# A two-layer hybrid block: tokens before the filters, and the convolutions of both lengths as one stream

## The chip, the cores and the metric

The kernel runs on one core of one Trainium2 chip. The metric is the device time of one execution in microseconds (us). TensorE is called PE in the profile (its weight loads PEld), VectorE DVE, ScalarE ACT, GpSimd POOL; SP is the engine that only issues DMAs. SP, ACT and POOL each issue their DMAs in the order in which they stand in that engine's instruction stream.

## The reference

Two layers of a token mixer and an MLP on 512 latent tokens and 256 context tokens of width 1024. Each sub-layer is modulated: a vector c (and one for the context) is multiplied with `w_mod`, and the result scales, shifts and gates the tokens. The mixer has four groups of 256 channels: a bidirectional state-space scan (SSD), a long convolution (Hyena), windowed attention and dense attention. What the change touches is the long convolution and its filters:

```python
def hyena_seq(u, conv_w, conv_b, spec, bias):
    n = u.shape[1]
    u = dw_conv_centred(u, conv_w, conv_b).astype(jnp.float32)
    v, x1, x2 = jnp.split(u, 3, axis=-1)
    gates = (x1, x2)
    z = v
    for o in range(HY_ORDER):            # HY_ORDER = 2
        zf = jnp.fft.irfft(jnp.fft.rfft(z, n=2 * n, axis=1) * spec[:, o], n=2 * n, axis=1)[:, :n]
        z = gates[o] * (zf + z * bias[o])
    return z
```

It is computed once for the 512 latent tokens in both layers and once for the 256 context tokens in layer 0 (layer 1 leaves the context out, since only the latents are returned). `spec` is the transform of an implicit filter: a small MLP with sines over positions, times a decay, normalised. The transforms are matrix products with constant tables of cosines and sines.

## The kernel before, in words

Everything is float32 in, float32 out. Most products are made of three matmuls in a reduced format (`mm3`, lines 296 to 300): each operand is split in a high part (`hi`, line 265 on ACT or 267 on DVE) and a low rest (`lo`, line 270 on DVE), and high by high, high by low and low by high are added in PSUM.

The program is written with pools of tiles: `push` opens a pool with so many buffers a tag, `a(tag)` takes the next one, `pop` closes it, and the place of a closed pool is used again by the next pool as soon as each tile in it is done with. A planner orders the instructions on each engine; its priority is the order in which they are written. `weave` (line 203) writes several generators in turn: in each round it runs n steps (to the next n yields) of each, with n given per generator. So a larger n puts a generator's work earlier.

The beginning (`run`, from line 1334). `filter_loads`, `filter_tables` and `filter_head` load the small filter weights and the tables on the queues of SP and POOL and compute the sine MLP. `pre` loads two token tiles of 128 x 1024 and normalises them; for the first pair this is done first, for the other two pairs after the weave. The weave runs `mod_cols` (two sections of `w_mod`, eight loads of 0.5 MB each on SP's queue with six buffers `wm`, and four small matmuls for each load, lines 447 and 449) with three steps a round beside `filter_seq(0, SEQ)` with two. `filter_seq` makes, for each of two orders, four filter tiles `kd` (lines 677 to 681), their sum and difference `ko` (696), transposes and splits them into `fx` (702, 704, 705), multiplies by the tables (716) and writes the spectra to DRAM through `fk` on POOL's queue (725). For layer 0 the large length has buffers of its own (`kd0`, `ko0`, `fx0`, `fk0`, in the pool `filL`). That pool is closed after the weave, and only then the pool of the transposed tokens (`push_xt`: tiles `xl` for the latents and `xc` for the context, high and low) is opened at its place. `pre_pair` (line 583) transposes the tokens on PE (593), applies the modulation (598) and splits them into `xl` and `xc` (267, 270). After that `filter_seq(1, SEQ)`, `filter_seq(0, CTX)` and the first projection to q, k and v (`qkv_in`, tiles `pg`) are written, then `layer` for each layer.

The middle of a layer (lines 1402 to 1423): SSD, long convolution and modulation are woven. `hyena` has 12 steps in each order for 512 tokens: two of transposes (802), four of forward products with a table each (`ht`, issued on POOL's queue, line 782), a product with the spectrum (`kt`, loaded on SP's queue at 816) and a split into `hu`, four of inverse products (847) with a table each (841), and two that add z (864) and multiply by the gate (866 or 868). For 256 tokens there are one, two, two and two. In layer 0 two such generators run in the weave, with one step a round each, beside SSD (one step) and four sections of `w_mod` (two steps, loads at line 447 into three buffers `raw`, which the weight loads share). They have separate tiles (`hx`, `hu`, `hxc`, `huc`) and banks (`ph2` one, `ph3` two, `pc` one), and share three table buffers `ht`. In layer 1 there is only the long length, with six buffers `ht` and two banks `ph2`, and no modulation. Behind the stage come `w_out` (tiles `py`, weights `wx` from line 348) and the MLP.

Of the kernel before, what the change touches and what calls it, by code (L numbers as in the profile page):

```python
# [12 lines left out]
F32 = mybir.dt.float32  # L13
# [9 lines left out]
SEQ = 512  # L23
# [141 lines left out]
W0 = (3, 2)  # L165
ME = (4, 1, 2)
EN = (("dve",), ("act", "dve"), ("dve",))
W2 = (1, 1, 2, 1)
# [15 lines left out]
class K:  # L184
# [420 lines left out]
    def filter_loads(self):  # L605
# [6 lines left out]
        zf = self.zf = self.a("fh")  # L612
# [4 lines left out]
        for l in range(DEPTH):  # L617
            r = slice(64 * l, 64 * l + 64)
            nc.sync.dma_start(w12[r, 1, r], A["hy_w2"][l])
        self.w3 = self.a("fw3")  # L620
        nc.sync.dma_start(self.w3, A["hw3"])

    def filter_head(self):
# [7 lines left out]
        for i in range(2):  # L631
            dst = self.a("fh")
# [23 lines left out]
    def filter_seq(self, l, n, tabs, v=""):  # L656
# [9 lines left out]
        for o in range(2):  # L666
            ss = self.sm(4, F32, "ss")
            kds = []
            for c in range(2):
# [4 lines left out]
                for d in range(2):  # L674
# [3 lines left out]
                    t = self.a("kd" + v)[:, :n]  # L678
# [12 lines left out]
            for cs in range(2):  # L691
                X = [self.a("fx" + v, (nb, 256)) for _ in range(2)]
                for c in range(2):
                    kd = kds[c]
                    src = self.a("ko" + v)[:, :n]
# [11 lines left out]
                for kc in range(h // 128):  # L707
                    p = self.a("pmod" if not v and kc % 2 else "pf3")
# [10 lines left out]
                    kt = self.a("fk" + v, (2, 256))  # L719
# [38 lines left out]
    def hyena(self, l, n, off, YT):  # L758
# [6 lines left out]
        v = "" if big else "c"  # L765
# [4 lines left out]
        def bank(tag):  # L770
            return self.a(tag if big else "pc")
        z = [self.a("hz" + v)[:, :n] for _ in range(2)]
        for c in range(2):
            nc.sync.dma_start(z[c], self.us_d[l][c][:, off:off + n])
        for o in range(2):
            ft = {}

            def ftab(sg, tcx, hl, kc):
                i = kc if big else 0
                if i not in ft:  # L780
                    ft[i] = self.a("ht")
                    nc.gpsimd.dma_start(ft[i], A["fwd%d" % n][i])
                if big:
                    c0 = 512 * sg + 256 * tcx + 128 * hl
                else:
                    c0 = 512 * sg + 256 * hl + 128 * kc
                return ft[i][:, c0:c0 + 128]

            pq = []
            for c in range(2):  # L790
                t = tmp((2, h))
                rev = z[c][:, n - 1:h - 1:-1]
                nc.vector.tensor_tensor(t[:, 0], z[c][:, 0:h], rev, ADD)
                nc.vector.tensor_tensor(t[:, 1], z[c][:, 0:h], rev, SUB)
                pq.append(t)
            X = []
            for sg in range(2 if big else 1):
                p = bank("ph3")
                for b in range(4):
                    c = b % 2  # L800
                    src = pq[c][:, sg, 128 * (b // 2):128 * (b // 2) + 128] if big else pq[c][:, b // 2, :]
                    nc.tensor.transpose(p[:, 128 * b:128 * b + 128], src, self.ident)
                x = self.a("hx" + v, (2, 512))
                self.hi(x[:, 0], p)
                self.lo(x[:, 1], p, x[:, 0])
                X.append(x)
                yield

            def xs(sg, tcx, hl):
                c0 = 256 * (tcx if big else sg)  # L810
                return X[sg if big else 0][:, hl, c0:c0 + 256]

            uv = []
            for kc in range(nk):
                kt = tmp((2, 256))
                nc.sync.dma_start(kt, self.spec[l, n][kc].rearrange("p (s o c) -> p s o c", s=2, o=2)[:, :, o, :])
                p = bank("ph2")
                for sg in range(2):
                    for tcx in range(nt):
                        self.mm3(p[:, 256 * sg:256 * sg + 256], ftab(sg, tcx, 0, kc), ftab(sg, tcx, 1, kc),  # L820
                                 xs(sg, tcx, 0), xs(sg, tcx, 1), tcx == 0, tcx == nt - 1)
                pv = p.rearrange("p (s c) -> p s c", s=2)
                a, b = tmp((2, 256)), tmp((2, 256))
                nc.vector.tensor_tensor(a, pv, kt[:, 0:1, :].to_broadcast([128, 2, 256]), MUL)
                nc.vector.tensor_tensor(b, pv, kt[:, 1:2, :].to_broadcast([128, 2, 256]), MUL)
                nc.vector.tensor_tensor(a[:, 0], a[:, 0], b[:, 1], SUB)
                nc.vector.tensor_tensor(a[:, 1], a[:, 1], b[:, 0], ADD)
                u = self.a("hu" + v, (2, 512))
                af = a.rearrange("p s c -> p (s c)")
                self.hi(u[:, 0], af)  # L830
                self.lo(u[:, 1], af, u[:, 0])
                uv.append(u)
                yield
            if big:
                ps = [bank("ph3") for _ in range(2)]
            else:
                p = bank("pc")
                ps = [p[:, 0:n], p[:, n:2 * n]]
            for kc in range(nk):
                tb = self.a("ht")  # L840
                nc.gpsimd.dma_start(tb, A["inv%d" % n][kc])
                tb = tb.rearrange("p (a b t) -> p a b t", a=2, b=2)
                for c in range(2):
                    for sg in range(2):
# [789 lines left out]
```

## Time and profile before

| | |
|---|---|
| median of 3 runs | 1918.94 us (1918.18 to 1923.98) |
| the profiled execution | 1919.0 us |
| its span, first to last instruction | 1917.2 us |
| mean granted clock of TensorE | 0.974 |
| busy: PE, PEld, DVE, ACT, POOL | 1790.2, 1482.7, 1297.7, 836.8, 91.5 us |
| DMA | 235.16 MB, mean 123 GB/s |

The busy times of the engines lie side by side, not one after the other. A PE row is the time of pipelined matmuls with modelled ends, so rows overlap. A row of the timeline merges equal instructions that follow each other (x6), and in brackets stands for how long the engine was idle before and what ended it. The chain of waits is followed back from the last instruction.

### The profile page before, as it was taken

What the parts mean: (1) busy time and instruction counts of PE and PEld (TensorE: products, weight loads), DVE (VectorE), ACT (ScalarE), POOL (GpSimd) and SP (SyncE); (2) the same over time, 40 slices, a digit from 0 to 9 for tenths busy, and PEclk for the clock granted to TensorE, in tenths of its full rate; (3) what the DMA queues carried; (4) which work ended last, traced back from release to release, by engine and by line L of the source; (5) the groups of instructions that cost most, each with busy time, mean ns of one, the idle gap of its engine ahead of it and who ended that gap; (6) DMA issues with size and microseconds to landing.
All of it is one profiled execution on the core that took longest, in us unless ns stands there. A gap on an engine that the chain in (4) does not pass through costs nothing.

```text
span 1917.2 us, 27370 instructions
## 1 busy us (share of the span) xinstructions
PE 1790.2 (93%) x10170; PEld 1482.7 (77%) x10170; DVE 1297.7 (68%) x2897; ACT 836.8 (44%) x1804; POOL 91.5 (5%) x176
## 2 busy tenths in 40 slices
PE   6899999978879999999999998899978789999998
PEld 2688888845668888888888888888866688888886
DVE  4878888877756656676666658988878563444446
ACT  4844565536515532322222327556546263332322
POOL 0120001011000000000000000000010000000000
PEclk9999999989989999999999999999989899999999
DMA  8531121278833244333333415112183243233232
GB/s 291 187 111 53 39 74 58 69 260 272 290 107 132 93 135 136 121 107 114 121 121 121 142 47 176 45 48 89 45 273 120 74 157 113 91 99 99 88 102 85
DMA packets 137597, 235.16 MB, mean 123 GB/s; under 512 B 12466, under 2 KB 77395, under 8 KB 137464
## 3 DMA queue, kind: packets, MB, share of 16 engines
q1 hardware_dynamic: 122920, 186.12, 30.2%
q0 software_dynamic: 14544, 47.30, 7.1%
q8 instruction: 80, 1.31, 0.3%
q14 instruction: 53, 0.43, 0.1%
HBM read 206.74 MB, written 26.64 MB: 122 GB/s over the span
## 4 chain that ended last, share of the span: by engine, by line
PE 76%; DVE 9%; issue 6%; DMA 4%; ACT 4%; POOL 1%; SPq 0%; DVEq 0%; ACTq 0%; POOLq 0%
PE pg L298 19%; PE pg L299 18%; PE pg L300 18%; PE po L1294 3%; PE py L298 2%; PE py L299 2%; PE pm L1286 2%; PE py L300 2%; PE ps L1249 1%; PE ps L1250 1%; PE pm L1206 1%; PE psd L1052 1%; DMA spec<-fk 1%; POOL spec L725 1%; DMA r<-in_w_mod_dram 1%
## 5 line engine op out<-in xcount | busy, mean ns | idle before, releaser
L265 ACT ACTIVATE w<-r 128x1024 fp32r<-128x1024 f32 (+1 forms) x176 | 186.6, 1061 | 348.1 <-PE pg L300 325.1
L270 DVE TENSOR_TENSOR w<-r,w 128x1024 fp32r<-128x1024 f32 (+1 forms) x176 | 214.1, 1223 | 106.1 <-ACT w L265 105.2
L298 PE MATMUL pg<-xl,w 128*128 128x512 f32 (+1 forms) x704 | 269.5, 386 | 2.2 <-DVE ya L1311 0.9
L300 PE MATMUL pg<-xl,w 128*128 128x512 f32 (+1 forms) x704 | 269.7, 384 | 0.0
L299 PE MATMUL pg<-xl,w 128*128 128x512 f32 (+1 forms) x704 | 269.7, 384 | 0.0
L298 PE MATMUL pg<-w,H 128*128 128x512 f32 x640 | 250.1, 391 | 0.0
L299 PE MATMUL pg<-w,H 128*128 128x512 f32 x640 | 249.2, 390 | 0.0
L300 PE MATMUL pg<-w,H 128*128 128x512 f32 x640 | 249.0, 389 | 0.0
L476 DVE SCALAR_TENSOR_TENSOR x<-r,scT,x 128x512 f32<-128x512 f32 x168 | 119.1, 746 | 71.7 <-DMA r<-in_w_mod_dram 71.7
L298 PEld LDWEIGHTS pg<-xl,w 128*128 128x128 f32 x704 | 132.6, 190 | 27.7 <-issue 2.2
L300 PEld LDWEIGHTS pg<-xl,w 128*128 128x128 f32 x704 | 133.3, 189 | 22.9
L299 PEld LDWEIGHTS pg<-xl,w 128*128 128x128 f32 x704 | 133.3, 189 | 22.2 <-DVE xl L270 0.2
L298 PEld LDWEIGHTS pg<-w,H 128*128 128x128 f32 x640 | 120.1, 188 | 26.8 <-issue 1.7
L300 PEld LDWEIGHTS pg<-w,H 128*128 128x128 f32 x640 | 120.1, 188 | 25.0
L299 PEld LDWEIGHTS pg<-w,H 128*128 128x128 f32 x640 | 120.2, 188 | 24.4
L1520 ACT ACTIVATE t<-pg 128x512 f32<-128x512 f32 (+1 forms) x100 | 50.4, 506 | 198.0 <-PE pg L300 198.0
L1551 DVE TENSOR_TENSOR ya<-pg,ya 128x512 f32<-128x512 f32 x120 | 81.8, 687 | 69.0 <-PE pg L300 68.7
L1522 DVE TENSOR_TENSOR t<-t 128x512 f32<-128x512 f32 (+1 forms) x100 | 58.1, 582 | 83.7 <-ACT H L1521 83.6
L300 PE MATMUL pg<-xc,w 128*128 128x256 f32 (+1 forms) x368 | 104.4, 284 | 0.0
L298 PE MATMUL pg<-xc,w 128*128 128x256 f32 (+1 forms) x368 | 103.3, 284 | 1.1 <-ACT xc L265 1.1
L299 PE MATMUL pg<-xc,w 128*128 128x256 f32 (+1 forms) x368 | 104.1, 284 | 0.0
L298 PE MATMUL pg<-w,xl 128*128 128x256 f32 (+1 forms) x320 | 93.0, 292 | 5.4 <-ACT qk L1113 2.5
(357 smaller groups left out, 3866.1 us busy)
## 6 DMA issues: line engine op xcount, KB each, us to landing
r<-in_mlp_w_dram SPq DMA_DIRECT2D x128, 512.0 KB
r<-in_w_mod_dram SPq DMA_DIRECT2D x80, 512.0 KB
r<-in_w_in_dram SPq DMA_DIRECT2D x40, 512.0 KB
ht<-in_inv_dram POOLq DMA_DIRECT2D x20, 512.0 KB, 5.4
ht<-in_fwd_dram POOLq DMA_DIRECT2D x18, 512.0 KB, 5.4
wm<-in_w_mod_dram SPq DMA_DIRECT2D x16, 512.0 KB
r<-in_w_out_dram SPq DMA_DIRECT2D x16, 512.0 KB
xd<-x POOLq DMA_DIRECT2D x16, 512.0 KB, 3.3
```

Source lines behind the costliest of these rows:

```text
L265: self.nc.scalar.activation(dst, src, AF.Copy)
L270: self.nc.vector.tensor_tensor(dst, src, h.bitcast(F32), SUB)
L298: mm(out, ah, bh, start=first, stop=False)
L299: mm(out, ah, bl, start=False, stop=False)
L300: mm(out, al, bh, start=False, stop=last)
L476: nc.vector.scalar_tensor_tensor(acc[:, c], raw[:, k], sc, acc[:, c], MUL, ADD)
L725: nc.gpsimd.dma_start(dst, kt[:, half, :])
L1286: nc.tensor.transpose(p[:, n:n + 128], P[:, col:col + 128], self.ident)
L1294: nc.tensor.matmul(po[:, qo:qo + m], V[:, c, :], pt[:, hl, cols[j]:cols[j] + m], start=i + j == 0 and hl == 0, stop=i + j == len(kts) - 1 ...
L1520: nc.scalar.activation(r, p[:, :nn], AF.Relu)
L1522: nc.vector.tensor_tensor(r, r, r, MUL)
L1551: nc.vector.tensor_tensor(dst, p, dst, ADD)
```

## The change

Three things change.

First, the beginning. The pool of the transposed tokens is opened before the filters' and has its own place; the large filter buffers (`kd0`, `ko0`, `fk0`, `fx0`) go, and all three calls of `filter_seq` use the small ones (four `kd`, two `ko`, one `fk`, three `fx`). All three pairs of token tiles are loaded and normalised first. The weave has two generators: the tokens (both sections of `w_mod`, then `pre_pair` for the three pairs: 18 and 3 steps) with six steps a round, and the filters (loads, then tables, head and `filter_seq(0, SEQ)`) with one. The input `zf` of the filter MLP takes one of the `raw` buffers.

Second, the convolutions. `hyena` becomes one generator over both lengths, in the order: 512 order 0, 256 order 0, 512 order 1, 256 order 1, with two steps a round in layer 0. Both lengths use the same tiles `hx` and `hu`, the same banks (`ph2` two, `ph3` two, `pc` is gone) and six table buffers `ht`. Layer 1 is as it was.

Third, the attention's `sqk` has five buffers instead of four.

The body of `hyena_order` is that of `hyena` for one order, but for the lines below.

```diff
-W0 = (3, 2)
+W0 = (6, 1)
-W2 = (1, 1, 2, 1)
+W2 = (1, 1, 2, 2)
...
-        zf = self.zf = self.a("fh")
+        zf = self.zf = self.raw_p.tile([128, 1024], F32, tag="r", name=self.nm("r"))[:, :NTOK]
+        self.h1 = self.a("fh")
-            dst = self.a("fh")
+            dst = self.a("fh") if i else self.h1
...
-    def filter_seq(self, l, n, tabs, v=""):
+    def filter_seq(self, l, n, tabs, two=True):
-                    t = self.a("kd" + v)[:, :n]
+                    t = self.a("kd")[:, :n]
-                X = [self.a("fx" + v, (nb, 256)) for _ in range(2)]
+                X = [self.a("fx", (nb, 256)) for _ in range(2)]
-                    src = self.a("ko" + v)[:, :n]
+                    src = self.a("ko")[:, :n]
-                    p = self.a("pmod" if not v and kc % 2 else "pf3")
+                    p = self.a("pmod" if two and kc % 2 else "pf3")
-                    kt = self.a("fk" + v, (2, 256))
+                    kt = self.a("fk", (2, 256))
...
-    def hyena(self, l, n, off, YT):
+    def hyena(self, l, lens, YT):
+
+        self.mark("hyena")
+        zs = {}
+        for n, off in lens:
+            zs[n] = [self.a("hz" if n == SEQ else "hzc")[:, :n] for _ in range(2)]
+            for c in range(2):
+                self.nc.sync.dma_start(zs[n][c], self.us_d[l][c][:, off:off + n])
+        for o in range(2):
+            for n, off in lens:
+                yield from self.hyena_order(l, n, off, YT, zs[n], o)
+
+    def hyena_order(self, l, n, off, YT, z, o):
...
-        v = "" if big else "c"
-        def bank(tag):
-            return self.a(tag if big else "pc")
...
-                p = bank("ph3")
+            p = self.a("ph3")
...
-                x = self.a("hx" + v, (2, 512))
+            x = self.a("hx", (2, 512))
...
-                p = bank("ph2")
+            p = self.a("ph2")
...
-                u = self.a("hu" + v, (2, 512))
+            u = self.a("hu", (2, 512))
...
-                ps = [bank("ph3") for _ in range(2)]
-            else:
-                p = bank("pc")
+            ps = [self.a("ph3") for _ in range(2)]
+        else:
+            p = self.a("ph3")
...
-        fl = self.push("filL", {"kd0": (512, F32, 8), "ko0": (512, F32, 4), "fk0": (512, F32, 2), "fx0": (1024, F32R, 4), "wm": (1024, F32, 6)})
-        self.filter_loads()
-        tb = self.filter_tables(SEQ)
-        self.filter_head()
+        XTp = self.push_xt()
+        fl = self.push("filL", {"wm": (1024, F32, 6)})
+        XT = self.new_xt()
-        xr = [pre(0)]
-        self.weave((chain(self.mod_cols(0, 0, 0), self.mod_cols(0, 1, 1, P_NMIX)), W0[0]),
-                   (self.filter_seq(0, SEQ, tb, "0"), W0[1]))
+        def tokens():
+
+            yield from self.mod_cols(0, 0, 0)
+            yield from self.mod_cols(0, 1, 1, P_NMIX)
+            for pair in range(3):
+                self.mark("pre")
+                self.pre_pair(xr[pair], pair, XT, self.mods[0, 1], self.mods[0, 0], EN[0])
+                yield
+
+        def filters():
+            self.filter_loads()
+            yield
+            self.tb = self.filter_tables(SEQ)
+            self.filter_head()
+            yield from self.filter_seq(0, SEQ, self.tb, False)
+        xr = [pre(pair) for pair in range(3)]
+        self.weave((tokens(), W0[0]), (filters(), W0[1]))
+        tb = self.tb
-        XTp = self.push_xt()
-        XT = self.new_xt()
-        xr += [pre(1), pre(2)]
-        for pair in range(3):
-            self.mark("pre")
-            self.pre_pair(xr[pair], pair, XT, self.mods[0, 1], self.mods[0, 0], EN[0])
-                                "QK": (768, F32R, 8), "pt": (1024, F32R, 2), "sqk": (256, F32R, 4)}, "right")
+                                "QK": (768, F32R, 8), "pt": (1024, F32R, 2), "sqk": (256, F32R, 5)}, "right")
-        hyt = {"hz": (512, F32, 2), "hf": (512, F32, SF[1] if need else SF[3]), "ht": (1024, F32R, 3 if need else 6), "hx": (1024, F32R, 2),
+        hyt = {"hz": (512, F32, 2), "hf": (512, F32, SF[1] if need else SF[3]), "ht": (1024, F32R, 6), "hx": (1024, F32R, 2),
-            hyt.update({"hzc": (256, F32, 2), "hxc": (1024, F32R, 1), "huc": (1024, F32R, 2)})
+            hyt["hzc"] = (256, F32, 2)
-        pp = self.push("ppB", {"ps": (512, F32, 1), "psd": (512, F32, 2), "ph2": (512, F32, 1 if need else 2),
-                               "ph3": (512, F32, 2), "pc": (512, F32, 1), "pg": (512, F32, 1)}, psum=True)
+        pp = self.push("ppB", {"ps": (512, F32, 1), "psd": (512, F32, 2), "ph2": (512, F32, 2),
+                               "ph3": (512, F32, 2), "pg": (512, F32, 1)}, psum=True)
-        hys = [(self.hyena(l, SEQ, 0, YT), W2[0])]
+        hy_ = (self.hyena(l, ((SEQ, 0), (CTX, SEQ)) if need else ((SEQ, 0),), YT), W2[3] if need else W2[0])
-        if need:
-            hys.append((self.hyena(l, CTX, SEQ, YT), W2[3]))
-        self.weave(*hys, (self.ssd(l, YT), W2[1]), (chain(*mods), W2[2]))
+        self.weave(hy_, (self.ssd(l, YT), W2[1]), (chain(*mods), W2[2]))
```

## Rows read from the trace of the kernel before

**Rows 1.** Stretches of the start: length, busy us and count of each engine, clock, DMA share, GB/s.
```profile
0.00:20.00 20.00, 3.65 (x5) 1.66 (x6) 4.02 (x13) 5.37 (x8) 3.54 (x12) 1.00 0.98 319
20.00:66.00 46.00, 44.21 (x286) 21.98 (x285) 33.90 (x122) 28.67 (x65) 5.39 (x10) 1.00 0.79 277
66.00:91.00 25.00, 17.58 (x111) 13.10 (x110) 21.38 (x65) 22.75 (x44) 3.22 (x6) 1.00 0.40 132
91.00:147.00 56.00, 53.19 (x395) 49.44 (x394) 40.35 (x128) 26.44 (x74) 13.45 (x25) 0.97 0.36 109
```
**Rows 2.** One tile's instructions, `xl`: count, duration min/median/max ns, first and last start.
```profile
L267 DVE CAST xl<-t x16: 282/284/293, 80.0 to 89.3; 128x256 fp32r<-128x256 f32 x16
```
**Rows 3.** The timeline of SP's queue, the start: start us, length us, engine, line.
```profile
9.03 2.03 SPq L1354 DMA_DIRECT2D w<-in_x_dram  x2
12.38 3.07 SPq L447 DMA_DIRECT2D wm<-in_w_mod_dram  x6
...
49.57 0.90 SPq L1354 DMA_DIRECT2D w<-in_x_dram  x2
50.52 0.90 SPq L1354 DMA_DIRECT2D w<-in_ctx_dram  x2
```
**Rows 4.** Stretches of the middle of layer 0, and that of layer 1.
```profile
393.00:543.50 150.50, 117.40 (x824) 79.20 (x823) 108.48 (x259) 73.17 (x216) 15.11 (x29) 0.86 0.79 264
...
393.00:530.00 137.00, 114.16 (x812) 76.74 (x811) 96.09 (x224) 69.10 (x208) 15.11 (x29) 0.88 0.86 287
...
1413.00:1500.00 87.00, 62.93 (x380) 49.48 (x381) 68.84 (x160) 46.63 (x137) 8.42 (x16) 0.87 0.54 179
```
**Rows 5.** One tile's instructions, `hz` (512 length), layer 0.
```profile
L793 DVE TENSOR_TENSOR hf<-hz x4: 415/416/418, 400.6 to 485.3; 128x256 f32<-128x256 f32 x4
...
L864 DVE SCALAR_TENSOR_TENSOR hf<-hz,pp,hf x4: 743/745/747, 464.5 to 534.8; 128x512 f32<-128x512 f32 x4
```
**Rows 6.** The same for layer 1.
```profile
L793 DVE TENSOR_TENSOR hf<-hz x4: 418/421/425, 1413.1 to 1464.8; 128x256 f32<-128x256 f32 x4
...
L864 DVE SCALAR_TENSOR_TENSOR hf<-hz,pp,hf x4: 742/746/750, 1453.1 to 1495.5; 128x512 f32<-128x512 f32 x4
```
**Rows 7.** The timeline of PE, its first matmuls.
```profile
13.59 2.90 PE L635 MATMUL pf<-fh,fw 33*128 33x512 f32 x4 [13.59 <-DMA fw<-in_hw_dram]
```
**Rows 8.** The timeline of POOL: spectrum steps 1, 8, 9, 16 and 20 of 20.
```profile
47.03 1.10 POOL L725 DMA_DIRECT2D spec<-fk  x2 [42.54 <-DVE fk L721]
...
76.20 1.07 POOL L725 DMA_DIRECT2D spec<-fk  x2 [3.17 <-DVE fk L721]
96.22 0.54 POOL L725 DMA_DIRECT2D spec<-fk  x1 [18.95 <-DVE fk L721]
...
124.96 1.07 POOL L725 DMA_DIRECT2D spec<-fk  x2 [2.56 <-DVE fk L721]
...
145.56 1.07 POOL L725 DMA_DIRECT2D spec<-fk  x2 [2.43 <-DVE fk L721]
```
**Rows 9.** The timeline of DVE: the norm of q and k begins.
```profile
155.17 0.17 DVE L293 TENSOR_SCALAR s<-dss 128x36 f32<-128x36 f32 x1
```
**Rows 10.** Idle time before instructions on `sqk`, layer 0: us, times.
```profile
  PE pm L1206: 9.9, 9
```
**Rows 11.** The chain of waits: start us, us, what.
```profile
509.17 5.95 DMA hf<-spec
517.44 4.09 DMA hf<-spec
...
543.50 0.80 PE py L298
...
1499.13 0.77 PE py L298
```
**Rows 12.** Who waited for whom, PE, 393 to 545 us: us, times, longest.
```profile
PE pc L298 <- DMA ht<-in_inv_dram: 3.5, 1, 3.5
...
PE ph L298 <- DMA ht<-in_inv_dram: 2.9, 1, 2.9
```

More of the change, by code (lines that the diff above doesn't have):

```diff
@@ new lines, in hyena_order, with xs @@
+        X = []
+        for sg in range(2 if big else 1):
+            p = self.a("ph3")
+            for b in range(4):
+                c = b % 2
+                src = pq[c][:, sg, 128 * (b // 2):128 * (b // 2) + 128] if big else pq[c][:, b // 2, :]
+                nc.tensor.transpose(p[:, 128 * b:128 * b + 128], src, self.ident)
+            x = self.a("hx", (2, 512))
+            self.hi(x[:, 0], p)
+            self.lo(x[:, 1], p, x[:, 0])
+            X.append(x)
+            yield
+        def xs(sg, tcx, hl):
+            c0 = 256 * (tcx if big else sg)
+            return X[sg if big else 0][:, hl, c0:c0 + 256]
@@ new lines, in hyena_order @@
+        for c in range(2):
+            gate = tmp((n,))
+            nc.sync.dma_start(gate, self.us_d[l][2 + 2 * o + c][:, off:off + n])
+            yv = tmp((n,))
+            p = ps[c]
+            if big:
+                dd = tmp((256,))
+                nc.scalar.activation(dd, p[:, 256:512], AF.Copy)
+                nc.vector.tensor_tensor(yv[:, 0:h], p[:, 0:256], dd, ADD)
+                nc.vector.tensor_tensor(yv[:, n - 1:h - 1:-1], p[:, 0:256], dd, SUB)
+                src = yv
+            else:
+                src = p
+            bias = self.pp[l][:, P_HBIAS + 2 * o + c:P_HBIAS + 2 * o + c + 1]
+            nc.vector.scalar_tensor_tensor(yv, z[c], bias, src, MUL, ADD)
+            if o == 0:
+                nc.vector.tensor_tensor(z[c], yv, gate, MUL)
+            else:
+                nc.vector.tensor_tensor(yv, yv, gate, MUL)
+                yh = cut(YT[0][2 + c], off, n)
+                self.hi(yh, yv, "dve")
+                self.lo(cut(YT[1][2 + c], off, n), yv, yh)
+            yield
```

133 lines of the change are left out of this document (48 added, 85 removed).

## The prediction, on record before the change was run

> **What bounds the kernel now.** I read the slices of the page first. PE is busy in 93% of the span, so most of the kernel, the MLP and the attention above all, can't be helped by an order of work. Two stretches are poorer, and the change touches just these two: the start, up to about 147 us, and the middle of layer 0, where convolutions, SSD and modulation run side by side. So I cut both into stretches and read the engines in each. At the start [rows 1] PE works 3.65 us of the first 20, nearly all of 20 to 66, only 17.58 of the 25 from 66 to 91, and 53.19 of the 56 after that. Its idle time is 16.35, 1.79, 7.42 and 2.81 us. The hole at 66 to 91 is explained by the token tiles: the first copy into `xl` is at 80.0 us [rows 2] and the first matmul that reads one comes after that, so until then PE has only the filters to do. The tiles are late since four of the six x loads stand on SP's queue behind the `w_mod` loads, at 49.57 us and later [rows 3], and since `xl` lies where the filter buffers were.
>
> In the middle of layer 0, 393.0 to 543.5 us, PE is busy 117.40 of 150.50 us, DVE 108.48, the DMA engines 0.79 of the time [rows 4]: nothing is full. In the same stage of layer 1, with one length and six table buffers but no modulation, 87 us pass [rows 4]. What runs through the whole stage in layer 0 is the chain of the 512 length: its first operation (line 793) is at 400.6, its last sum with z (line 864) starts at 534.8, so 134.2 us [rows 5]. In layer 1 the same chain takes 1413.1 to 1495.5, 82.4 us [rows 6]. The question is how much of these 51.8 us the new order gives back, with 14 steps of the other length now in the same chain.
>
> The sum is made against the profiled execution, 1919.0 us (span 1917.2 and 1.8 around it); the median of the three runs is 1918.94, the same. A measurement of this kernel can tell about 0.3%, 5.8 us, from no change.
>
> **The start.** Removed: the wait of the tokens for the place of the filters, and the late x loads. All six x loads now go out before the first `w_mod` load. Four move up, 4 x 0.512 MB. The first 20 us moved 319 GB/s [rows 1], so this puts off what is behind them by 2.1 MB / 319 GB/s = 6.4 us. The small filter loads moved behind these and, as the woven order has six token steps before the first filter step, behind six `w_mod` loads too (3.1 MB, 9.9 us). Today the first filter matmul starts at 13.59 us, as its load has landed [rows 7]. It moves by something between 0 (if the loads interleave) and 6.4 + 9.9 = 16.3 us. I take 12, nearer to the upper end, because the queue of SP issues in order. The four kernel tables go out on POOL's queue, which has nothing else to issue before the spectra, so their move costs nothing. The pre-norms of the two later pairs, eight long operations, move ahead of the filters on ACT, which is busy only 5.37 of the first 20 us and 28.67 of the next 46 [rows 1].
>
> Does that matter? The filter chain sends a spectrum step off every few us: the first of 20 at 47.03, the eighth at 76.20, then, after a hole, the ninth at 96.22, the sixteenth at 124.96 and the last at 145.56 [rows 8]. The sixteenth less the ninth gives 28.74 / 7 = 4.1 us a step, with the small buffers that now serve all 20 steps (the first eight, with twice the buffers, took 29.17 / 7 = 4.2 us, so halving them costs nothing by these rows). The hole of 20.0 us is when the tokens are scaled and split on ACT and DVE; less one step it is 15.9. After the change, 19 intervals of 4.1 are 78 us. If the first step leaves at 47 + 12 = 59 and the hole falls wholly into the time in which the filters wait for their loads anyway, the last leaves at 137; if it comes in full, at 153. I take the middle, 145, which is today's 145.56. So the filters end when they end now. The gain is that the projection of q, k and v no longer competes with their last steps: it can fill PE from about 66 us on instead of after 91. Today the norm of q and k begins at 155.17 us [rows 9], 9.6 after the last spectrum step. If only the last 5 us of that remain, 4.6 us go; PE's idle 7.42 + 2.81 = 10.2 us is the most that can come back. Against this stands PE's later start, at least 0 and, by the loads, at most 16.3 us, hidden as far as the filter chain is hidden. I take -3, between -10 and +9.
>
> **The fifth `sqk` buffer.** Writes into `sqk` wait 9.9 us in nine pieces for PE to release a tile in layer 0 [rows 10], but PE is nearly full in that stage, so most of it is hidden: between -9.9 and 0, I take -1.
>
> **The middle of layer 0.** The arithmetic is the same: the same matmuls, 22 tables of 0.5 MB, the same `w_mod`. The order and the buffers change. The chain now is the 512 length's order 0, the 256 length's order 0, then both again: 24 + 14 = 38 steps in one stream, two a round. Term by term:
> - the 24 steps of the 512 length, with six table buffers, as layer 1 shows them: 82.4 us, 3.43 a step [rows 6].
> - the 14 steps of the 256 length: half the columns in most operations, so between 14 x 3.43 / 2 = 24 and 14 x 3.43 = 48 us. I take the middle, 36. They partly fill the waits of the other length, but share `ph3`, `hx` and `hu` with it, so I don't count that twice. The wait that is added is the short length's transposes on a `ph3` bank, until DVE has read the long one's result; behind them on PE stand matmuls of SSD and of the modulation, which DVE's splits and the `w_mod` loads wait for. In today's trace the long length has its own banks, so this wait has no row; its place in the 24 to 48 us holds it.
> - what layer 1 doesn't have: `w_mod` loads ahead of the spectra on SP's queue. The chain of waits shows 5.95 + 4.09 us of waiting for spectra at its end [rows 11]. They stay: 10 us. At the least 0.
> - sum 82.4 + 36 + 10 = 128.4 against 134.2: -6. With the ends, 106 to 140, -28 to +6.
> - the tail. Now 543.50 - 534.8 = 8.7 us pass from the last sum to the first output matmul [rows 5, 11], for DVE first finishes the long convolution, the SSD norm of the context and weight splits. In layer 1 it is 1499.13 - 1495.5 = 3.6 [rows 6, 11]. After the change the last piece is the short length, SSD is some rounds ahead, and the place of the weight tiles is free earlier. I take -4, between -5 and 0.
>
> So -10 for the stage. The six buffers themselves remove 3.5 + 2.9 us in which PE waited for a table [rows 12]; that is part of the step price of layer 1, not added. The second `ph2` bank is in that price too. What is late next are the transfers: from 393 to 530 us they run at 287 GB/s with the DMA engines 0.86 busy [rows 4], so they alone want 0.86 x 137 = 118 us, and with the 6 us of a short tail and some 4 us of start the stage can't give more than about 22.
>
> The Trainium skill speaks against the extra buffers here (DMA: Bandwidth & Descriptors, section "Issuing engines are not separate DMA queues"): transfers started from different engines run on the same 16 DMA engines and interleave, so tables that POOL requests earlier take their time from the loads on SP's queue. The 0.86 agrees with it; if every early table only put off a `w_mod` load, the stage would keep its length but for the tail, and the sum would be 1911 instead of 1905. The same skill (Perfetto Trace Analysis, section "Identifying the Most-Contended Engine") calls the matmul row a poor measure and weight loads a better one: 79.20 of 150.50 us here, by which PE would bound the stage even less than the 117.40 say.
>
> Sum: 1919.0 - 3 - 1 - 10 = 1905 us.
>
> **Rivals.**
> 1. *One stream is slower than two* (slower). The 38 steps follow each other through two `ph3` banks and four `hu` tiles, and each step's spectrum waits behind `w_mod` loads. For: order 1 of the long length ran today at (534.8 - 485.3) / 12 = 4.1 us a step [rows 5] although nothing of the short one was left beside it. At that price for all steps the chain is 38 x 4.1 = 156 us, 21.8 more than 134.2; with the shorter tail and the start, 1919 + 21.8 - 4 - 3 - 1 = 1933. It decides from 134.2 / 38 = 3.53 us a step, just above layer 1's 3.43. Against: a step of the short length has half the columns, and with 31 equivalent steps even 4.1 gives 127, a gain. Chance 0.14.
> 2. *The start loses what the middle gains.* The loads put the filter chain off by the full 12 to 16 us and the tokens stall it again: last step at 153 to 157, +9; the middle gives -9: 1919. For: the first 20 us have the DMA engines 0.98 busy [rows 1], so no load can be early without another being late. Against: those holes in PE at 66 to 91. Chance 0.18.
> 3. *The start's hole closes in full and the middle goes down to its transfers*: -10 and -20 (near the 22 of the transfers), so 1889. For: nothing is full in either stretch. Against: neither engine order nor queues are ideal today, and both remain in-order. Chance 0.13.
>
> **Chances and range.** My forecast has 0.55; its own range is 1895 to 1913. The likeliest time is 1905; the range that leaves out 2 in 10 is 1887 to 1924, which takes in most of rival 3 and of rival 2, and not rival 1. Faster by more than 5.8 us: 0.55 x 0.97 + 0.13 + a little of rival 2 = 0.68. Within 5.8: 0.16, nearly all rival 2. Slower: rival 1 and a part of rival 2, 0.16.
>
> **What would show it.** In the profile after: the six x loads ahead of the first `w_mod` load; the first copy into `xl` near 60 us instead of 80.0, PE nearly full from 66 to 91; the first spectrum write at 55 to 62 and the last at 140 to 152. In the middle: no more PE waits for tables, order 0 of the long length done some 50 us after its start, the short one's last sum at the end of the stage, output matmuls within 5 us of it, and the whole stage some 140 us. I am wrong if the stage in layer 0 is not shorter than 145 us, if the filters' last write is later than 155 us, or if the time before the attention grows.

## The result and the profile after

The changed kernel took 1947.68 us (median of four runs, 1947.32 to 1951.74), the kernel before 1919.8 beside it: ratio 1.0147, 95% interval 1.0125 to 1.0168. It is 28 us slower, where 14 faster was forecast and 1887 to 1924 was the range. The profiled execution has a span of 1949.9 us, 32.7 more than before.

The span splits at three places that every kernel here has: the first transposes of q and k (tile `pm`), the last write of the attention (`yy`) and the first output matmul (`py`).

| us | before | after | difference |
|---|---|---|---|
| start, 0 to `pm` | 169.6 | 190.8 | +21.2 |
| attention of layer 0, to the last `yy` | 225.8 | 225.0 | -0.8 |
| middle of layer 0, to `py` | 148.1 | 157.4 | +9.2 |
| the rest | 1373.7 | 1376.8 | +3.1 |

The start by stretches, as in [rows 1]: length, then busy time of PE, PEld, DVE, ACT and POOL, granted clock (1.00 is 2.4 GHz, 0.50 is 1.2), DMA share, GB/s.

```profile
0.00:20.00 20.00, 0.28 (x2) 0.29 (x2) 2.91 (x19) 6.52 (x10) 3.53 (x12) 1.00 0.95 339
20.00:66.00 46.00, 34.49 (x206) 14.35 (x205) 26.33 (x97) 29.58 (x55) 0.00 (x0) 0.76 0.77 267
66.00:91.00 25.00, 23.95 (x150) 19.98 (x149) 20.10 (x52) 14.37 (x31) 3.23 (x6) 0.90 0.32 95
91.00:147.00 56.00, 53.53 (x364) 45.34 (x363) 40.59 (x114) 27.45 (x69) 13.24 (x25) 1.00 0.33 100
```

The hole at 66 to 91 closed, as forecast: 23.95 of 25 us busy, not 17.58. But a larger one opened ahead of it, 34.49 of 46 where 44.21 stood, and the clock there is 0.76 instead of 1.00. The timelines of SP and PE show the head of the filters, which was at 13.59 [rows 7]:

```profile
8.86 8.66 SPq L447 DMA_DIRECT2D wm<-in_w_mod_dram  x6
18.46 0.33 SPq L610 DMA_DIRECT2D s<-in_pf_dram  x1
...
29.12 2.14 PE L636 MATMUL pf<-r,fw 33*128 33x512 f32 x4 [0.42 <-DMA fw<-in_hw_dram]
```

The tokens are early (first copy into `xl` at 54.96, in [rows 2] 80.0). The spectrum writes on POOL's timeline, steps 1, 8, 9, 16 and 20, answer [rows 8]:

```profile
79.00 1.09 POOL L726 DMA_DIRECT2D spec<-fk  x2 [74.53 <-DVE fk L722]
...
109.86 1.07 POOL L726 DMA_DIRECT2D spec<-fk  x2 [2.65 <-DVE fk L722]
114.90 1.07 POOL L726 DMA_DIRECT2D spec<-fk  x2 [3.96 <-DVE fk L722]
...
151.34 1.07 POOL L726 DMA_DIRECT2D spec<-fk  x2 [4.19 <-DVE fk L722]
...
169.16 1.07 POOL L726 DMA_DIRECT2D spec<-fk  x2 [5.24 <-DVE fk L722]
```

The last is 23.6 us later than before, and `pm` comes 21.6 us behind it (24.0 before). The middle from the last `yy` to `py`, before and then after, with the chain of waits of after (answers to [rows 4, 11]):

```profile
395.40:543.50 148.10, 115.00 (x805) 76.85 (x804) 106.42 (x255) 72.62 (x215) 14.92 (x28) 0.86 0.79 265
```
```profile
415.80:573.10 157.30, 117.31 (x798) 76.86 (x796) 106.82 (x251) 73.58 (x216) 14.88 (x28) 0.84 0.76 250
```
```profile
425.23 12.07 DMA sy<-xb
439.24 9.28 DMA hf<-spec
454.07 7.21 DMA hf<-spec
...
504.97 7.67 DMA hf<-spec
```

PE does the same work and is idle 7 us longer; the waits for spectra behind `w_mod` loads are 24.2 us in this chain, 10 were counted.

### The profile page after: what moved, and what is told of

It is laid out like the page before. It is cut to its first block, busy times and chain, and to the rows that moved or that the text cites. A ratio compares the mean times of both kernels' runs of the same rounds, so it can differ in the third digit from the quotient of the medians.

```text
span 1949.9 us, 27386 instructions
## 1 busy us (share of the span) xinstructions
PE 1799.5 (92%) x10170; PEld 1488.5 (76%) x10170; DVE 1297.6 (67%) x2897; ACT 838.8 (43%) x1804; POOL 91.5 (5%) x176
## 4 chain that ended last, share of the span: by engine, by line
PE 74%; DVE 10%; DMA 7%; issue 5%; ACT 3%; POOL 1%; SPq 0%; DVEq 0%; ACTq 0%; POOLq 0%
PE pg L298 18%; PE pg L299 18%; PE pg L300 18%; PE po L1300 3%; DMA r<-in_w_mod_dram 2%; PE pm L1292 2%; PE py L300 2%; PE py L298 2%; PE py L299 2%; PE ps L1255 2%; DMA hf<-spec 1%; PE pm L1212 1%; PE ps L1256 1%; DVE w L270 1%; DMA spec<-fk 1%
```

## The experiments

Ratios are to the kernel before, run beside each on the same chip; the square brackets hold 95% intervals.

### Which part loses

The two parts alone. The start alone leaves out the hunks of `hyena`, of its tiles and banks and of `sqk`; the middle alone leaves out those of the start and of `sqk`:

```diff
# start alone, against the changed kernel
-W2 = (1, 1, 2, 2)
+W2 = (1, 1, 2, 1)
-"sqk": (256, F32R, 5)
+"sqk": (256, F32R, 4)
...
# middle alone, against the changed kernel
-W0 = (6, 1)
+W0 = (3, 2)
...
```

> Only the start of the change (own place for the token tiles, x loads first, filters woven behind the tokens with small buffers); the middle stays two streams with three tables and four sqk tiles. Theory A (the start costs what the trace shows there: pm of the first attention 21.2 us later): about 1939 us, +20 on the 1919.8 of before. Theory B (the delay of the start is made good before the attention ends, and the loss is all in the middle): 1919 to 1925.

> Only the middle of the change (both lengths in one stream, six table buffers, weight 2); start and sqk as before. Theory A (the middle loses some 10 us of its own, since the short length's chain got 9 us longer): about 1930. Theory C (the middle's own effect is the forecast gain and its loss comes only from the later start): about 1909. Rival 1 of the prediction (4.1 us for each of the 38 steps): 1937.

Start alone: 1955.22, ratio 1.0169 [1.0135, 1.0204]. Middle alone: 1926.26, ratio 1.0026 [1.0006, 1.0046]; its middle takes 148.0 us, as before. So the start carries the loss, and more than theory A of the first run gave it (1939). In the second theory C falls, and of A the stage shows nothing: by itself the new order neither gives nor costs time there:

```profile
399.80:547.80 148.00, 114.19 (x805) 74.62 (x803) 106.98 (x252) 73.95 (x216) 14.92 (x28) 0.87 0.80 264
```

The 4 us of its span are older than the middle: its first spectrum write is at 51.4, not 47.03, with no line of the start edited. From 25 to 34.5 us, in the kernel before and then in the middle alone:

```profile
25.00:34.50 9.50, 9.50 (x60) 2.84 (x58) 5.23 (x19) 5.24 (x11) 0.00 (x0) 1.00 0.51 167
25.00:34.50 9.50, 9.50 (x37) 2.75 (x36) 2.65 (x7) 4.25 (x8) 0.00 (x0) 1.00 0.38 133
```

Both rows give the clock as 1.00, but a matmul of the modulation takes 587 to 634 ns in the second and 377 to 379 in the first; the mended kernel below takes 584 to 635 where its rows give 0.50. So here the row does not tell the slower clock. The kernel before leaves it at 24.4 us and the middle alone at 34.8, with the same order of instructions on PE there. Differences of some 4 us between the starts of two single traces can therefore be this and not the edit.

The start alone has 235.0 us of attention, 10 more than the changed kernel (by the marks used here, not the 225 and 218 of the next expectation); the run with four `sqk` tiles says why:

```diff
-"sqk": (256, F32R, 5)
+"sqk": (256, F32R, 4)
```

> The changed kernel with four sqk tiles, as before, instead of five. By the two profiles the attention of layer 0 takes 225 us with four (start of the change alone) and 218 with five (the changed kernel): if that is the fifth tile, 1954, 7 more than the changed kernel. If it is only the planner's order, the same within 0.3%.

1954.03, ratio 1.0174 [1.0153, 1.0194], some 5 us above the changed kernel's, though the intervals overlap; the attention takes 234.1 us. Behind the new start the fifth tile is worth 9 us there, of which 3.5 are lost again in the middle (157.4 with five, 153.9 with four). Behind the old start the attention takes 225.8 us with four tiles; five were not run there.

### Order of the loads and weights

```diff
# loads first, against the changed kernel
+        self.filter_loads()
+        self.tb = self.filter_tables(SEQ)
+        self.filter_head()
         def filters():
-            self.filter_loads()
-            yield
-            self.tb = self.filter_tables(SEQ)
-            self.filter_head()
# and with other weights (two runs); weights alone (one run)
-W0 = (6, 1)
+W0 = (3, 2)      # or (1, 2)
```

> The changed kernel with one thing put back: the small filter loads, the four kernel tables and the filter head are issued before the x loads, not as the first two steps of the filters' share of the weave. Theory L (the loss at the start is the order of the loads: filter head at 29.12 instead of 13.59): the head comes back to some 14 us, the first spectrum write to some 60 and the whole to about 1932, 15 us less than the 1947.7. Theory P (the filter chain is held up by the tokens' pre-norm and scaling, woven with weight 6 to 1 ahead of it on DVE and ACT): the head is early, but the first spectrum write stays later than 72 and the time above 1942.

> The changed kernel with the filters' loads, tables and head ahead of the x loads, and with the old weights of the weave (three token steps to two filter steps, instead of six to one). Theory F (the start is as long as the filter chain: its first write, 19 steps of 4 to 5 us, and some 22 us to the first transposes of the attention, whose banks take the place of the filters'; loads and weights only move its beginning): first spectrum write at 47 to 60, the last at 140 to 150, first transposes of q and k at 163 to 172, the whole at 1918 to 1930. Theory P (own place and small buffers are themselves slow: the tokens on DVE and ACT slow each filter step): the last write stays later than 155 and the whole above 1938.

> As the run before, with one token step to two filter steps: the filters are written ahead. Theory F: first write at 45 to 50, the last at 127 to 145 as the tokens fill what the chain leaves; the attention begins at 150 to 168 and the whole is 1900 to 1925. Rival (then the tokens and the projection of q, k and v are late and end the start): the last write is early, but the attention begins after 172 and the whole is above 1930.

> The changed kernel with only the weights put back to three token steps to two filter steps; the filters' loads stay behind the x loads. Theory L (order of the loads): the head stays at some 20 to 29 us, and the whole within 5 us of the changed kernel's 1947. Theory F with the weights as the main cause: first write at 60 to 70, the last at 150 to 160, the whole 1930 to 1940.

| | ratio | first write | last write | `pm` |
|---|---|---|---|---|
| loads first, 6:1 | 1.0126 [1.0091, 1.0161] | 85.3 | 165.2 | 188.1 |
| loads first, 3:2 | 1.0126 [1.0103, 1.0149] | 53.2 | 161.8 | 186.0 |
| loads first, 1:2 | 1.0154 [1.0132, 1.0176] | 48.5 | 163.4 | 188.4 |
| 3:2 alone | 1.0108 [1.0088, 1.0127] | 55.6 | 158.1 | 181.1 |

Theory L's forecast falls: the head is at 13 us again in the first three and nothing is won that the intervals tell from the changed kernel's; with 6:1 and with 3:2 the signs of theory P came. But these runs do more than bring the head back, as the next part shows on SP's queue: they hold up `w_mod` loads, so the price of a late head alone stays open. The weights alone give some 7 us, by intervals that just touch; the time lies above the range of theory F. With the filters first (1:2) the first write is as early as before, yet the last is 18 us later. Theory F holds in one half only: `pm` follows the last write by 19 to 25 us in all twenty kernels, but an early first write does not bring an early last one. Something had made the filter steps longer.

### The filter buffers

Three single edits to the kernel before, then two that split the first:

```diff
# small buffers (cut: the entries of the pool go too)
-t = self.a("kd" + v)[:, :n]        # ko, fx, fk likewise
+t = self.a("kd")[:, :n]
# own place: small buffers, and
+        XTp = self.push_xt()       # ahead of push("filL")
# x loads first
-        xr = [pre(0)]
+        xr = [pre(pair) for pair in range(3)]
# only fk single
-kt = self.a("fk" + v, (2, 256))
+kt = self.a("fk", (2, 256))
# small kd, ko, fx; fk0 keeps its two
```

> The kernel before with one edit: the first filters use the small buffers (four kd, two ko, one fk, three fx instead of eight, four, two, four more of their own). The prediction put this at nothing. Theory B (the large buffers carry the first eight steps beside the modulation): these steps take 36 to 40 us instead of 29, the last write comes some 8 us later and the whole is about 1928 to 1932. Prediction: 1919 to 1923.

> The run with small buffers, and the token tiles in a place of their own; the order in which things are written stays that of before (filters' loads first, one pair of tokens loaded early, tokens scaled after the weave). If the own place lets the tokens fill holes of PE, 3 to 10 us less than the run with small buffers alone; if the tokens wait for their scales and loads anyway, the same within 0.3%.

> The kernel before with one edit: all three pairs of token tiles are loaded and normalised before the weave. Theory X (2 MB more ahead of the w_mod loads put the modulation off by 6.4 us, and the pre-norms take DVE and ACT from the filters): the last filter write is 4 to 8 us later and the whole 1923 to 1929. Rival (the w_mod loads are not what the start waits for): 1919 to 1921.

> The kernel before with one edit: the first eight filter steps write their spectra through the single fk of the later steps, not through two of their own; kd, ko and fx keep their large number. Theory K (the single fk is the price of the small buffers: VectorE waits for each write to land, and with it all that stands behind): 1931 to 1937, as with all buffers small. Theory N (kd, ko and fx are what lets filters run ahead): 1919 to 1924.

> The kernel before with small kd, ko and fx, but two fk of their own for the first eight steps. Theory K: 1919 to 1925. Theory N: 1931 to 1937.

| | ratio | eighth write | last write | `pm` |
|---|---|---|---|---|
| before | 1 | 76.2 | 145.6 | 169.6 |
| small buffers | 1.0071 [1.0049, 1.0093] | 86.7 | 161.4 | 185.5 |
| own place too | 1.0074 [1.0051, 1.0097] | 87.6 | 163.2 | 187.2 |
| x loads first | 1.0065 [1.0040, 1.0090] | 83.3 | 152.8 | 176.8 |
| only fk single | 1.0060 [1.0041, 1.0080] | 84.1 | 155.0 | 180.0 |
| small kd, ko, fx | 1.0041 [1.0026, 1.0056] | 79.8 | 153.9 | 177.9 |

Small buffers alone cost 13.7 us (0.71% of 1922.9), as much as half of the loss and above theory B's range. Their first eight steps take 40.6 us from first write to eighth (46.1 to 86.7), where the kernel before takes 29.2. The place costs nothing further and gives nothing. Both K and N get a part: the single `fk` 11.5 us, the three others 7.9, together less than the sum. The x loads ahead of the `w_mod` loads cost 12 us: the last write is 7.2 us later, inside the 4 to 8 expected, and the whole, 1937.56, above the 1923 to 1929. Its twelve runs lie apart, two at 1921 (mean granted clock 0.971 and 0.973), ten between 1930 and 1946 (0.960 to 0.971), and the profile is one of the former, so it shows only a part of what the latter lose. That part is on SP's queue:

```profile
14.39 0.91 SPq L447 DMA_DIRECT2D wm<-in_w_mod_dram  x2
27.67 0.33 SPq L673 DMA_DIRECT2D dec<-in_decay_dram  x1
28.04 2.33 SPq L447 DMA_DIRECT2D wm<-in_w_mod_dram  x5
```

SP stands at a load of the filters' decay (`dec`, two buffers) until VectorE has used an earlier one, 11.9 us of waiting in one piece. It stands so in the kernel before too, but there six `w_mod` loads have gone out ahead of it [rows 3] and here two. So the next four leave at 28 us and later, not by 15, and the last at 51.1 and not 41.3: more than the 6.4 us that the bytes would cost. All kernels with the filters' loads and all x loads ahead of the weave show it (loads first: two at 14.28, the next at 29.23). The changed kernel does not: six leave from 8.86 on, the last at 39. So this delay is no part of its loss, but it is in the kernels with loads first and in the mended one. No run moves the `dec` load.

What a single `fk` does, in the run with small buffers: VectorE's timeline, and what it waited for from 40 to 90 us (total, times, longest).

```profile
49.97 0.69 DVE L270 TENSOR_TENSOR fx<-pf,fx 128x512 fp32r<-128x512 f32 x1 [2.03 <-PE pf L299]
53.68 0.42 DVE L721 TENSOR_TENSOR fk<-pf,t 128x256 f32<-128x256 f32 x1 [3.02 <-DMA spec<-fk]
54.02 0.41 DVE L722 TENSOR_TENSOR fk<-pf,t 128x256 f32<-128x256 f32 x1
54.35 0.68 DVE L270 TENSOR_TENSOR fx<-pf,fx 128x512 fp32r<-128x512 f32 x1
```
```profile
DVE fk L721 <- DMA spec<-fk: 7.5, 4, 3.3
```

The same wait in the kernel before:

```profile
DVE fk L721 <- DMA spec<-fk: 0.4, 1, 0.4
```

At 50.7 VectorE is free, but the next spectrum tile is the one that is still being written to DRAM, and the split into `fx` at 54.35, which PE needs, stands behind it. In the changed kernel these waits come to 12.9 us in ten pieces.

The Trainium skill (DMA: Bandwidth & Descriptors, section "Anatomy of one DMA — SWDGE (gpsimd) path") puts most of a fixed cost of about 2 us into the receipt of the last byte's landing. The trace agrees with the size: the changed kernel's writes landed 2.0 to 4.9 us after their issue, 2.3 in the median; what part of it is the receipt no run shows.

The other half of the price is the clock. From 0 to `pm`, before, with small buffers, and in the changed kernel:

```profile
0.00:169.60 169.60, 137.88 (x948) 105.03 (x948) 120.02 (x381) 91.63 (x210) 25.60 (x53) 0.99 0.53 175
```
```profile
0.00:185.50 185.50, 147.89 (x948) 112.42 (x948) 120.87 (x381) 92.13 (x210) 25.51 (x53) 0.90 0.49 160
```
```profile
0.00:190.80 190.80, 147.38 (x976) 113.28 (x977) 124.90 (x386) 95.38 (x213) 25.50 (x53) 0.92 0.49 160
```

The same 948 matmuls keep PE busy 10.0 us longer with small buffers, with a granted clock of 0.90 and not 0.99 (a 128x128 transpose takes 420 ns where the rows give 0.50, 283 at 1.00), and PE is idle 37.6 instead of 31.7 us. These two are the 15.9 us by which `pm` is late. Of the 10.4 us with only `fk` single they are 5.8 and 4.6, of the 8.3 with small `kd`, `ko` and `fx` 6.6 and 1.7 (clock 0.95 and 0.94). That the waits are what brings the clock down is argued, not shown.

### Taking the wait away

```diff
# in the changed kernel, all 20 steps; in the kernel before, the last 12 alone (cut)
-kt = self.a("fk", (2, 256))
+kt = self.t2((128, 2, 256))
```

> The changed kernel with the spectrum tile taken from the ring of five short-lived tiles in all 20 filter steps, instead of the single fk. Theory K: the 12.9 us of waits for spec<-fk go, the last write comes 8 to 12 us earlier and the whole is 1935 to 1941. Theory N, or the ring waits just as long: within 0.3% of 1947.

> The kernel before with the spectrum tile of the later twelve filter steps in the ring of five short-lived tiles; the first eight keep their two. There VectorE waits 3.6 us in three pieces for the write to land. Theory K: 2 to 4 us less, 1915 to 1918 against 1919 to 1922. Otherwise the same.

Changed kernel: 1943.04, ratio 1.0109 [1.0091, 1.0128]. The waits are gone, the last write comes at 159.4 and `pm` at 178.9, 12 us earlier, as theory K wants, and the whole stays 2 us above its range: 5 us of that go again in the attention (230.0) and 3 in the rest (1379.9), 5 come in the middle (152.4). Kernel before: 1918.32, ratio 0.9975 [0.9961, 0.9988], so 4.8 us faster, and the one version here that beats both. Its trace does not show that beside the kernel before's (`pm` at 172.1), since its matmuls, too, take the slower time until 34.5 us; beside the middle alone, whose start is that of before and as slow to begin, the last write is 2.7 us earlier (147.0 against 149.7) and `pm` 1.7.

### The middle behind the new start

```diff
# three tables in layer 0
-"ht": (1024, F32R, 6)
+"ht": (1024, F32R, 3 if need else 6)
# hz, hzc, sb and sy of layer 0 on ACT's queue
-nc.sync.dma_start(xc, ...
+(nc.scalar if l == 0 else nc.sync).dma_start(xc, ...
# sb of layer 0 on POOL's queue
-nc.sync.dma_start(bt, self.xb_d[l][2])
+(nc.gpsimd if l == 0 else nc.sync).dma_start(bt, self.xb_d[l][2])
```

> The changed kernel with three table buffers in layer 0 instead of six; one stream stays. Theory T (six tables of 0.5 MB go out at once ahead of the SSD's first loads and put the stage off): the SSD's first matmuls are earlier and the whole gives back 4 to 8 us, 1940 to 1944. Theory H (what holds the stage is the one serial chain and its spectra behind the w_mod loads on SP): the same within 0.3%, 1947, or a few us more, as PE waits for tables again.

> The changed kernel with three of the middle's loads in layer 0 (hz and hzc, sb, sy) on ACT's queue instead of SP's, where a w_mod load that waits for its buffer stands ahead of them. Theory Q (the middle of the changed kernel takes 157 us and not the 148 that the same code takes in the run of the middle alone, because SP is held at its beginning): SSD's first load comes 7 us earlier against the last attention write, the stage takes 148 to 152 and the whole 1939 to 1943. Rival R (the whole stage runs in another order that is slower all along): the stage stays at 154 or more, the whole within 0.3% of 1947.

> The changed kernel with one edit: in layer 0 the load of sb goes on POOL's queue, so that SSD's first two loads come before it on SP. Theory S (the middle's 7 to 9 us are lost at its beginning, where SSD's first matmul is 16.9 us behind the last attention write instead of 8.5 to 9.4): that distance falls to 12 or less, the stage to 149 to 153 us, the whole to 1939 to 1943. Rival R (it is the whole order that is slower): the distance falls and the stage stays at 155 or more, the whole within 0.3% of 1947.

Three tables: 1947.57, ratio 1.0137 [1.0100, 1.0173], as theory H says. Of theory T one half came: SSD's first matmul is 13.5 us behind the last `yy`, not 16.9, and the stage 154.0. The Trainium skill's rule that all queues share the same DMA engines (DMA: Bandwidth & Descriptors, section "Issuing engines are not separate DMA queues") is seen in the chain above, 12.07 us for a `sy` load issued behind five tables (the sixth goes out 1.2 us later), with the DMA engines full; but three fewer gave no time back in the whole. ACT's queue: 1954.56, ratio 1.0166 [1.0140, 1.0192], the stage 162.9; the first `sy` load is no earlier (8.4 us behind the last `yy`, 7.3 in the changed kernel), and ACT stood 10.4 us at one place with DMAs to issue, so the run tells nothing of theory Q. POOL's queue: 1947.69, ratio 1.0134 [1.0115, 1.0154]. SSD's first matmul is 11.9 us behind the last `yy` (16.9 in the changed kernel), and the stage is as long as it was:

```profile
413.90:570.80 156.90, 116.12 (x799) 75.35 (x798) 107.67 (x252) 73.73 (x216) 15.42 (x29) 0.86 0.76 251
```

Theory S falls. What the runs do show: the stage is 146.5 to 151.0 us in the eight kernels whose tokens are scaled behind the old weave, and 152.4 to 162.9 in the twelve with tokens and filters in the new weave, with either order in the middle (154.8 with the old one). SP's timeline shows that the planner has put the loads of the stage in another order: middle alone, then changed kernel.

```profile
397.48 0.82 SPq L765 DMA_DIRECT2D hz<-us  x2
398.35 1.06 SPq L765 DMA_DIRECT2D hzc<-us  x2
399.51 0.37 SPq L994 DMA_DIRECT2D sy<-xb  x1
402.01 0.33 SPq L447 DMA_DIRECT2D r<-in_w_mod_dram  x1
408.05 0.32 SPq L981 DMA_DIRECT2D sb<-xb  x1
```
```profile
417.40 0.34 SPq L447 DMA_DIRECT2D r<-in_w_mod_dram  x1
417.83 0.86 SPq L766 DMA_DIRECT2D hz<-us  x2
418.74 1.50 SPq L766 DMA_DIRECT2D hzc<-us  x2
422.64 0.32 SPq L982 DMA_DIRECT2D sb<-xb  x1
423.07 0.91 SPq L995 DMA_DIRECT2D sy<-xb  x2
```

That the order is the cause is argued, not shown; which piece of it costs the 6 to 9 us stays open.

### Mended

Spectrum tile in the ring, loads first, weights 3:2 and `sb` on POOL's queue, the edits of above together.

> The changed kernel with four edits: spectrum tile in the ring of five, filters' loads, tables and head ahead of the x loads, weights three to two, and sb on POOL's queue. If the start is mended by the first three, the attention begins at 172 to 178 instead of 190.8; with theory S the whole is 1922 to 1932, otherwise 1930 to 1938. Rival P (own place and kd, ko, fx in small number cost the rest): the attention begins after 180 and the whole stays above 1935.

1940.34, ratio 1.0099 [1.0082, 1.0116]; `pm` at 181.2, the last write at 156.0. The signs of rival P came; that own place and small `kd`, `ko` and `fx` are the cause is not shown, since this kernel also holds four `w_mod` loads behind `dec` until 27.25 us, and the place cost nothing above. The stretches from 25 to 50 us and from 0 to `pm`, then the first of before:

```profile
25.00:50.00 25.00, 23.32 (x111) 8.32 (x113) 12.82 (x49) 14.84 (x26) 0.00 (x0) 0.50 0.66 232
0.00:181.20 181.20, 150.76 (x948) 110.96 (x948) 121.04 (x381) 91.95 (x211) 25.49 (x53) 0.89 0.50 164
```
```profile
25.00:50.00 25.00, 24.14 (x168) 10.24 (x166) 17.54 (x58) 14.27 (x34) 1.10 (x2) 1.00 0.74 263
```

PE is idle 30.4 us, a little less than the 31.7 of before, and still `pm` is 11.6 us late: the whole of it is 12.9 us more in the same 948 matmuls. From 25 to 50 us PE looks busy in both, but at 1.2 GHz it gets through 111 matmuls and not 168.

## Why the prediction was wrong

**The start, forecast -3, measured +21.2.**
- *Head put off by 12, at most 16.3.* It was 15.5, inside the bounds. What it costs alone stays open: the runs that bring it back hold up `w_mod` loads instead.
- *First write at 47 + 12 = 59.* It came at 79.0. The working moved the head and forgot what now stands ahead of the chain on DVE and ACT: from head to first write 49.9 us instead of 33.4. With three token steps to two, the head still late, it is 30.5 (25.08 to 55.6), so the weights make it.
- *"Halving them costs nothing by these rows."* This is the step that failed most: 13.7 us by the run that does only that. The rows compared steps 1 to 8 with steps 9 to 16 and found 4.2 and 4.1 us each. But the rows had more than the number of buffers changed. The modulation's matmuls run beside the first of these steps, until 54 us, and steps 9 to 16 take every second product in a second bank, `pmod`, which the first eight do not have:

```profile
L721 DVE TENSOR_TENSOR fk<-pmod,t x4: 415/422/425, 99.5 to 124.3; 128x256 f32<-128x256 f32 x4
```

Which of the two hid the price is not shown. The 0.4 us of waits for `spec<-fk` with two buffers, and the 3.6 us with one from 90 to 150 us, were in the trace to be read.
- *19 intervals of 4.1.* They were 90.2 / 19 = 4.75. The last write at 145 came at 169.2, beyond the 155 named as proof of error.
- *PE fills from 66 us on.* True, and worth nothing: `pm` kept its 19 to 25 us behind the filters' last write in every kernel.
- No term stood for the clock. With small buffers it goes with 10.0 of 15.9 us.
- How the start's 21.2 us add up stays open. Small buffers alone put `pm` off by 15.9; in the changed kernel the ring, which takes back one of these buffers, gives 11.9, and the weights put back give 9.7. No run undoes buffers and weights together with the loads left as they are.

**`sqk`, forecast -1.** In this kernel it is worth -2.3 us by the spans and about -5 by the ratios; behind the old start it was not run.

**The middle, forecast -10, measured +9.2, of which the edit itself about 0.** Middle alone: the chain from the first operation on `hz` to the short length's last sum is 135.8 us, not 128.4; the tail 7.0, not 4.7. Against 134.2 and 8.7 before, these are +1.6 and -1.7. The first operations (798) and last sums (869) of both lengths, and the long one's first in order 1:

```profile
L798 DVE TENSOR_TENSOR hf<-hz x4: 414/416/417, 405.1 to 466.4; 128x256 f32<-128x256 f32 x4
L869 DVE SCALAR_TENSOR_TENSOR hf<-hz,pp,hf x4: 732/738/753, 449.5 to 516.9; 128x512 f32<-128x512 f32 x4
L798 DVE TENSOR_TENSOR t<-hzc x4: 270/277/282, 451.4 to 505.3; 128x128 f32<-128x128 f32 x4
L869 DVE SCALAR_TENSOR_TENSOR t<-hzc,pp,ph x4: 473/475/479, 472.1 to 540.9; 128x256 f32<-128x256 f32 x4
464.42 0.41 DVE L798 TENSOR_TENSOR hf<-hz 128x256 f32<-128x256 f32 x1
```

The long length holds 46.3 (405.1 to 451.4) and 52.5 us (464.4 to 516.9), the short one the 37.0 between and behind. The short one was counted at 36; the mis-sized term is the long one, 98.8 against 82.4 from layer 1 and 10 for spectra. Layer 1 has neither modulation nor a second length beside it. So rival 1's condition came, 135.8 / 38 = 3.57 us a step against its limit of 3.53, but not its price of 4.1, and the stage stayed as long. The six tables did remove PE's waits for tables [rows 12], which the stage does not show.

**The rivals.** Rival 2 named the place (filters late, tokens in their way) but at +9, from the loads and the tokens' stall. None had buffers or clock as its mechanism, so the range ended 24 us short.

## What to carry to other kernels

Price a buffer by the waits on it in a stretch where the same work runs beside the same company, and look first at tiles that a DMA reads, since a single one stops an in-order engine until the write has landed. An order that feeds PE less well can also leave it at half clock: in a stretch count matmuls, and look at the time of one, not busy time alone. On an in-order queue look for a load that waits for a buffer, and for what an edit puts behind it. A change at the start can reorder, through the planner, a stage that it doesn't touch, so test each part alone.

## What the runs showed of the hardware

PE need not stand idle for long to be at 1.2 GHz. In the changed kernel, 20 to 30 and 30 to 40 us, it was 6.65 and 7.43 of 10 us busy, and its longest pause from 22 to 30 us was 1.27 us:

```profile
20.00:30.00 10.00, 6.65 (x58) 2.46 (x57) 4.15 (x27) 8.32 (x11) 0.00 (x0) 0.99 1.02 359
30.00:40.00 10.00, 7.43 (x45) 2.37 (x43) 3.00 (x7) 3.83 (x7) 0.00 (x0) 0.50 1.00 382
```

And it can stay there while busy, as the mended kernel's 23.32 of 25 us at 0.50 show. At the beginning of a trace the row of the clock can read 1.00 while matmuls take the time that they take at 0.50 (middle alone, until 34.8 us; loads first, until 47).
